# A decoder layer whose ring of gathered expert rows borrows tiles that are not yet in use

## The chip, the cores and the metric

The kernel runs on one core of one Trainium2 chip. The metric is the device time of one execution in microseconds (us); less is better. Several runs of the same program are listed and their median counts.

## The reference

The reference is one layer of a decoder for 512 tokens of 1024 features, in 32-bit floats. Its first half mixes tokens by two groups of heads: sparse attention over a shared latent, where an indexer chooses 128 keys for each query, and a gated linear recurrence in chunks of 32 tokens. An output projection, a residual and a layer norm follow; the result is called h here. Its second half is a product-key layer of 16384 experts, each of one neuron: every token chooses 16 experts for each of 8 heads, 128 in all.

```python
def _peer(x, w_q, sub_keys, u, v):
    ...
    def one_block(xb):
        q = (xb @ w_q).reshape(PEER_BLOCK, PEER_HEADS, 2, PEER_KEY_DIM // 2)
        s = jnp.einsum('thpd,hpkd->thpk', q, sub_keys).astype(jnp.float32)
        s_top, i_top = lax.top_k(s, K)
        ...
        best, pos = lax.top_k(cand.reshape(PEER_BLOCK, PEER_HEADS, K * K), K)
        experts = jnp.take_along_axis(...)
        g = jax.nn.softmax(best, axis=-1).astype(xb.dtype)
        h = jax.nn.gelu(jnp.einsum('td,thkd->thk', xb, u[experts]))
        return jnp.einsum('thk,thkd->td', g * h, v[experts])
    ...
def reference(...):
    ...
        h = _layer_norm(ALPHA * x + mix, ln1_g[layer], ln1_b[layer])
        ffn = _peer(h, peer_w_q[layer], peer_sub_keys[layer], peer_u[layer], peer_v[layer])
        x = _layer_norm(ALPHA * h + ffn, ln2_g[layer], ln2_b[layer])
```

## The kernel before

The 512 tokens are four blocks of 128, a token on each partition. `stage([0])` computes the mixing half and the choice of experts for block 0 alone; `stage([1, 2, 3])` does the same for the other three blocks together. Blocks 0 and 1 get their experts by gathering: row k of a block is a tile of 128 x 1024 floats (512 KB) that holds, for each of the 128 tokens, its k-th expert's line of `u` or `v`. Blocks 2 and 3 are computed densely against all experts at the end (`dense`): 128 steps stream all of `u` and `v` through TensorE.

**Rows.** `gather` (L625) takes a tile from the ring "g" of four buffers (`GB = 4`) and lets POOL issue an indirect DMA into it. `peer_gather(b)` (L645) gathers 128 rows of `u`, each multiplied with h and summed by one DVE instruction (L651), and then rows of `v`, each added to the block's sum by one DVE instruction (L664): 128 + 76 rows for block 0, since 52 of its `v` rows go to TensorE later (`pe_gather`), and 128 + 128 for block 1. These DVE instructions are pinned by `keep_in_program_order` behind the DVE instruction traced just before them. `pump(n)` works off n rows at fixed places of the program; the table `PUMP` gives n for each place. In `stage([1, 2, 3])` the places before the mixing norm pump 8 (cw) + 16 (qi) + 24 (sel) + 60 (the four projections of the recurrence) + 30 (hgrn) + 8 (qa) + 24 (att) = 170 rows of block 0; the mixing norm pumps 8 more, and the first quarter of the queries the last 26. Then come 14 rows on TensorE, 38 more in the dense stage, and the rows of block 1, spread over the dense loop.

**Tiles that the change touches.** The pool `cst` lives as long as the kernel. `hsA` and `hsB` (L169, L170) hold x, then h, of two blocks each: 2 x 4 KB on each partition. `hTh` (L171) and `hTl` (L865) are the high and low parts of h transposed, for blocks 2 and 3, 8 KB each; `hTl` takes the place of `hsB` once h is transposed. `mix_norm` (L470) loads x of its blocks by SP (L474), multiplies by the output weights `wo` in two halves (L486), adds (L489) and norms. For blocks 1 to 3 the homes of x are empty until then, and that of `hTh` until the queries are done (L869, L870).

**What sets the order.** All instructions are traced in program order; then a planner with a timing model of its own lays them out, engine by engine, taking the earliest traced instruction that its model holds ready. A tile's buffer must be released by all users of its last tenant before a new tenant is written. Each engine and each DMA queue then runs its list in order: POOL the gathers, SP all other loads, waiting at the head of the list where need be.

Of the kernel before, what the change touches and what calls it, by code (L numbers as in the profile page):

```python
# [9 lines left out]
F32 = mybir.dt.float32  # L10
# [14 lines left out]
DENSE = (2, 3)  # L25
# buffers of the rings of tiles
HGB = 5
# [6 lines left out]
PJ = 16  # L34
# rows of experts worked off at each such place of the program (sel: one at every second step)
PUMP = {"cw": 4, "qi": 4, "hf": 4, "hq": 4, "hi": 4, "hg": 3, "qa": 2, "hgrn": 1, "att": 4, "mix": 1, "sel": 2,
        "q0": 7, "q1": 0, "q2": 0, "q3": 0}
# rows of block 0's sum that the tensor engine takes: after the queries, and beside the dense weights
PEK1 = 14
PEK2 = 38  # L40
PEPRE = 8
PEG = 60
# tokens of each four whose weights ScalarE multiplies in
GACTS = (3, 4)
# a row of experts at every so manyth group of the dense weights
GPUMP = 3
# the dense step by which all rows are worked off
DLAST = 127
# [3 lines left out]
def tile_decoder_layer(ctx, tc, a, out):  # L52
# [70 lines left out]
    def layer_norm(ys, os_, g, b, nm):  # L123
        """Each y is a tile or a list of its parts along the features."""
        n = len(ys)
        mv = cst.tile([128, n, 2], F32, name="mv" + nm, tag="ln_mv", bufs=2)
        parts = [y if isinstance(y, list) else [y[:, k * 512:(k + 1) * 512] for k in range(2)] for y in ys]
        for i in range(n):
            st = cst.tile([128, 2, 6], F32, name=f"st{nm}_{i}", tag="ln_st", bufs=2)
            for k in range(2):  # L130
                nc.vector.bn_stats(st[:, k, :], parts[i][k])  # L131
            nc.vector.bn_aggr(mv[:, i, :], st)
        ve = cst.tile([128, n], F32, name="ve" + nm, tag="ln_ve", bufs=2)
        nc.vector.tensor_scalar(ve, mv[:, :, 1], EPS, None, op0=ALU.add)
        r = rsqrt(ve, n, nm)
        for i, o in enumerate(os_):
            if isinstance(ys[i], list):
                for k in range(2):
                    sl = slice(k * 512, k * 512 + 512)
                    nc.vector.scalar_tensor_tensor(o[:, sl], parts[i][k], mv[:, i, 0:1], g[:, sl],  # L140
                                                   op0=ALU.subtract, op1=ALU.mult)
            else:
                nc.vector.scalar_tensor_tensor(o, ys[i], mv[:, i, 0:1], g, op0=ALU.subtract, op1=ALU.mult)  # L143
            nc.vector.scalar_tensor_tensor(o, o, r[:, i:i + 1], b, op0=ALU.mult, op1=ALU.add)  # L144
# [23 lines left out]
    kiT = pre.tile([128, 512], F32, name="kiT")  # L168
    hsA = cst.tile([128, 2, 1024], F32, name="hsA")  # L169
    hsB = cst.tile([128, 2, 1024], F32, name="hsB", tag="hsB")  # L170
    hTh = cst.tile([128, 8, 256], F32R, name="hTh")  # L171
    hs = [hsA[:, 0, :], hsA[:, 1, :], hsB[:, 0, :], hsB[:, 1, :]]
    idx = [[cst.tile([128, 64], U32, name=f"idx{b}_{n}") for n in range(2)] for b in range(2)]
# [5 lines left out]
    def tok_major(blocks, xT, w, name):  # L179
        """x W for each block, tokens on partitions."""  # L180
        ps_ = [bank(f"{name}{b}") for b in blocks]
        n = w.shape[-1]
        step = 2 if n == 512 else 4
        for k0 in range(0, 8, step):
            wt = stream(f"{name}w{blocks[0]}_{k0}", w[:, k0:k0 + step, :])
            pump(PUMP[name])
            for i in range(len(blocks)):
                for k in range(step):
                    nc.tensor.matmul(ps_[i][:, :n], xT[:, k0 + k, i * 128:(i + 1) * 128], wt[:, k, :],
                                     start=(k0 + k == 0), stop=(k0 + k == 7))  # L190
        return ps_

    def feat_major(blocks, xT, w, name):
        """(x W)^T for all blocks at once, features on partitions: a bank for each 128 features."""
        m = w.shape[-1] // 128
# [22 lines left out]
    def lower_bound():  # L218
# [6 lines left out]

        # lower bound of the forget gate: f = fa + fc * tanh(z / 2)
        fa = pre.tile([128, 512], F32, name="fa")
# [41 lines left out]
    def hgrn(b, pr, mixT):  # L269
# [35 lines left out]
        for par in range(2):  # L305
            ap_ = bank(f"at{b}_{par}", "hg")
            for j in range(4):
# [3 lines left out]
                                    tri[:, None, :].to_broadcast([128, 4, 128]), op=ALU.mult)  # L311
        # the states before each chunk of 32
        S = []
# [86 lines left out]
    def select(b, pr):  # L400
        """What to add to the negated attention scores of the keys that the index doesn't choose."""
        nk = (b + 1) * 128
# [67 lines left out]
    def mix_norm(blocks, mixT):  # L470
        ys = {}
        for b in blocks:
            ys[b] = hs[b]
            tc.keep_in_program_order(nc.sync.dma_start(ys[b], a["x"][b * 128:(b + 1) * 128, :]))  # L474
# [18 lines left out]
    def queries(blocks, hT):  # L493
        """Sub-key scores and, for each of the 16 lists, its 16 best."""
        nt = 128 * len(blocks)
# [53 lines left out]
    def best16(b, g, sv, si, bv, pos):  # L549
        # a pair (a, b) can be among the 16 best only if (a + 1) * (b + 1) <= 16; the places keep the pairs' order  # L550
        s4 = sv[:, g * 4:g * 4 + 4, :].rearrange("p (h z) k -> p h z k", z=2)
# [15 lines left out]
    def routing(b, half, sv, si, bv, pos):  # L567
        """The experts and their weights for four of the block's heads."""
        H = slice(half * 4, half * 4 + 4)
        C = slice(half * 64, half * 64 + 64)  # L570
        # place -> the two ranks
        p2 = pos[:, H, :].rearrange("p h k -> p (h k)")
# [20 lines left out]
        nc.vector.tensor_copy(rbb, t1)  # L593
        # rank -> sub-key
        si4 = si.rearrange("p (h z) k -> p h z k", z=2)
# [18 lines left out]
        if b not in DENSE:  # L614
            nc.vector.scalar_tensor_tensor(idx[b][half], val[1], 128.0, val[0], op0=ALU.mult, op1=ALU.add)
        # softmax over the 16 kept, whose first is their maximum
        g3 = gate[:, b, C].rearrange("p (h k) -> p h k", h=4)
# [5 lines left out]
        nc.vector.tensor_tensor(g3, g3, gsum[:, :, None].to_broadcast([128, 4, 16]), op=ALU.mult)  # L623

    def gather(table, b, k, nm):  # L625
        t = gat.tile([128, 1024], F32, name=f"g{nm}{b}_{k}", tag="g", bufs=GB)
        nc.gpsimd.indirect_dma_start(out=t, out_offset=None, in_=table,  # L627
                                     in_offset=bass.IndirectOffsetOnAxis(ap=idx[b][k // 64][:, k % 64:k % 64 + 1], axis=0))
        return t
# [15 lines left out]
    def peer_gather(b):  # L645
        """Yields True after each row of experts is worked off, False where it waits for pe_gather."""
        hd = cst.tile([128, 128], F32, name=f"hd{b}", tag="hd")
# [24 lines left out]
    def pe_gather(n, p):  # L672
        """A part of block 0's sum over the rows of v on the tensor engine: diag(weight) @ rows; yields after each."""
        while 0 not in weighted:
# [27 lines left out]
    def dense(den, dps):  # L702
        """Tokens of the DENSE blocks against every expert, with the experts' weights scattered to a dense matrix."""
        nb = len(DENSE)
        T = 128 * nb
        tr = {}
        hTl = consts_loaded["hTl"]
        for i, b in enumerate(DENSE):
# [56 lines left out]
        def into_hidden(j, n, hp):  # L765
# [3 lines left out]
            for q, (ut, ht) in enumerate(((uh, hTl), (uh, hTh), (ul, hTh))):  # L769
                for k in range(4):  # L770
                    nc.tensor.matmul(hp, ut[:, k * 128:(k + 1) * 128], ht[:, n * 4 + k, :],  # L771
                                     start=(n + q + k == 0), stop=(n == 1 and q == 2 and k == 3))
# [20 lines left out]
        def residual():  # L793
            ia = gat.tile([128, 128], F32, name="ia", tag="dg", bufs=1)
            nc.scalar.mul(ia, ident, ALPHA)
            for i in range(nb):
                for n in range(2):
                    for c in range(4):
                        for t in (hTl, hTh):
                            nc.tensor.matmul(acc[i][n][:, c * 128:(c + 1) * 128],  # L800
                                             t.bitcast(F32)[:, n * 4 + c, i * 128:(i + 1) * 128], ia,
                                             start=False, stop=False)
# [29 lines left out]
    def stage(blocks, xT):  # L832
# [31 lines left out]
        if blocks != [0]:  # L864
            hTl = cst.tile([128, 8, 256], F32R, name="hTl", tag="hsB")  # L865
            consts_loaded["hTl"] = hTl
            for k in range(0, 8, 2):
                x = hT[:, k:k + 2, 128:384]
                nc.scalar.copy(hTh[:, k:k + 2, :], x)  # L869
                nc.vector.tensor_tensor(hTl[:, k:k + 2, :], x, hTh[:, k:k + 2, :].bitcast(F32), op=ALU.subtract)  # L870
            for _ in pe_gather(PEK1, [bank(f"pv{i}", "hg") for i in range(2)]):
                pass
# [56 lines left out]
```

## Time and profile before

| | us |
|---|---|
| three runs | 1656.95, 1659.08, 1651.08 |
| median | 1656.95 |
| profiled execution, first to last instruction (span) | 1647.0 |
| PE, DVE, ACT, POOL busy in it | 1456.9, 1387.7, 706.5, 663.7 |

For the profiled execution the page gives the span alone; its time by the clock of the runs isn't listed, and the median lies 9.95 us above the span. The engines are PE (TensorE), DVE (VectorE), ACT (ScalarE), POOL (GpSimd) and SP (SyncE, which issues DMAs). In the page's 40 slices of 41 us a digit is a share in tenths:

```profile
PE   8889899763577899868998999999999999999996
...
DVE  4139899787787669998887899998999899999998
...
POOL 0003423456665251135443344443444345534540
PEclk9899899755599999989999999999999999999998
DMA  7377878788887785246677999999999999999995
```

Block 0's stage ends at about 140 us (slice 4). Up to slice 16 the other three blocks are projected, selected, run through recurrence and attention and normed, with block 0's rows in between; then come queries, routing and the scatter of weights, and from slice 21 the dense loop. A busy share says how full an engine is, not what sets the end; for that one asks each engine what ended its idle time.

### The profile page before, as it was taken

The page shows a single profiled execution, that of the slowest core. Times are in us where ns is not written, and L with a number is a line of the kernel's source. Part 1 is how long each engine was busy: PE and PEld are TensorE (multiplying, and loading weights), DVE is VectorE, ACT ScalarE, POOL GpSimd, SP SyncE. Part 2 cuts the span into 40 slices and gives each one's busy share as a digit, 9 for nine tenths or more (in the row PEclk, how much of TensorE's full clock was granted, in tenths as well). Part 3 has the DMA queues.
Part 4 walks back from the last instruction along what each step waited for, and adds up shares of the span by engine and source line. Part 5 has one row for each costly group of instructions (what it writes and reads, how often), then busy time and mean ns, then how long its engine had stood idle before and what let it go on. Part 6 is the DMA issues. An engine that isn't in the chain of part 4 may idle for free. (4 is left out here: it accounts for less than half of the span.)

```text
span 1647.0 us, 24505 instructions
## 1 busy us (share of the span) xinstructions
PE 1456.9 (88%) x7858; PEld 1096.3 (67%) x7858; DVE 1387.7 (84%) x3263; ACT 706.5 (43%) x1501; POOL 663.7 (40%) x531
## 2 busy tenths in 40 slices
PE   8889899763577899868998999999999999999996
PEld 4567444542333365425667888888888889989885
DVE  4139899787787669998887899998999899999998
ACT  3312321122233010327996555555555555555553
POOL 0003423456665251135443344443444345534540
PEclk9899899755599999989999999999999999999998
DMA  7377878788887785246677999999999999999995
GB/s 284 122 275 248 280 265 290 245 273 275 262 276 252 264 306 186 84 136 226 220 218 263 327 345 351 355 345 344 343 356 344 336 347 359 365 349 345 354 358 191
DMA packets 166161, 467.89 MB, mean 284 GB/s; under 512 B 18576, under 2 KB 18704, under 8 KB 165904
## 3 DMA queue, kind: packets, MB, share of 16 engines
q0 software_dynamic: 73728, 268.47, 48.0%
q1 hardware_dynamic: 92304, 197.86, 33.2%
q8 instruction: 62, 1.02, 0.2%
q14 instruction: 67, 0.55, 0.1%
HBM read 464.16 MB, written 2.10 MB: 283 GB/s over the span
## 5 line engine op out<-in xcount | busy, mean ns | idle before, releaser
L627 POOL DMA_INDIRECT gv<-in_v_dram,idx x256 | 335.1, 1309 | 420.0 <-DVE hsA L664 268.6
L627 POOL DMA_INDIRECT gu<-in_u_dram,idx x256 | 318.6, 1245 | 458.2 <-DVE gu L651 289.3
L651 DVE SCALAR_TENSOR_TENSOR gu<-gu,hsA 128x1024 f32<-128x1024 f32 x256 | 309.5, 1225 | 52.5 <-DMA gu<-in_u_dram,idx 51.9
L664 DVE SCALAR_TENSOR_TENSOR hsA<-gv,gate,hsA 128x1024 f32<-128x1024 f32 x204 | 261.6, 1282 | 30.0 <-DMA gv<-in_v_dram,idx 26.6
L760 ACT CAST v_0h<-v 128x512 fp32r<-128x512 f32 x128 | 79.7, 622 | 96.7 <-PE acc L791 55.4
L518 PE MATMUL pq<-hT,wpq 128*128 128x128 f32 (+1 forms) x512 | 118.8, 390 | 0.0
L760 ACT CAST v_1h<-v 128x512 fp32r<-128x512 f32 x128 | 79.5, 621 | 88.6 <-DMA v<-in_v_dram 45.7
L762 DVE TENSOR_TENSOR u_0l<-u,u_0h 128x512 fp32r<-128x512 f32 x128 | 88.5, 692 | 32.7 <-ACT u_0h L760 29.9
L760 ACT CAST u_0h<-u 128x512 fp32r<-128x512 f32 x128 | 79.4, 620 | 72.2 <-PE hp L771 40.1
L791 PE MATMUL acc<-v_0h,wl 128*128 128x512 f32 x256 | 101.9, 398 | 2.5 <-DVE wl L781 2.5
L518 PEld LDWEIGHTS pq<-hT,wpq 128*128 128x128 f32 x512 | 80.0, 198 | 32.1 <-issue 1.7
L762 DVE TENSOR_TENSOR v_1l<-v,v_1h 128x512 fp32r<-128x512 f32 x128 | 87.8, 686 | 15.8 <-ACT v_1h L760 13.5
L791 PE MATMUL acc<-v_0h,wh 128*128 128x512 f32 x256 | 101.0, 394 | 0.0
L791 PE MATMUL acc<-v_1h,wl 128*128 128x512 f32 x256 | 99.7, 389 | 0.0
L791 PE MATMUL acc<-v_1h,wh 128*128 128x512 f32 x256 | 99.7, 389 | 0.0
L791 PE MATMUL acc<-v_0l,wh 128*128 128x512 f32 x256 | 99.5, 390 | 0.0
L760 ACT CAST u_1h<-u 128x512 fp32r<-128x512 f32 x128 | 79.4, 621 | 46.4 <-PE acc L791 42.3
L735 DVE TENSOR_TENSOR og<-iota,dtr 128x512 f32<-128x512 f32 x128 | 81.6, 687 | 13.6 <-PE gb L744 11.7
L762 DVE TENSOR_TENSOR u_1l<-u,u_1h 128x512 fp32r<-128x512 f32 x128 | 87.8, 686 | 5.1 <-ACT wh L779 2.7
L762 DVE TENSOR_TENSOR v_0l<-v,v_0h 128x512 fp32r<-128x512 f32 x128 | 88.0, 688 | 3.4 <-ACT v_0h L760 2.1
L682 PE MATMUL pw<-gv,dg 128*128 128x512 f32 x152 | 76.0, 623 | 15.6 <-ACT dg L680 9.1
L771 PE MATMUL hp<-hTl,u_0h 128*128 128x256 f32 x512 | 84.3, 287 | 5.8 <-ACT u_0h L760 5.8
(282 smaller groups left out, 3166.6 us busy)
## 6 DMA issues: line engine op xcount, KB each, us to landing
v<-in_v_dram SPq DMA_DIRECT2D x256, 256.0 KB
u<-in_ut_dram SPq DMA_DIRECT2D x256, 256.0 KB
wpq<-in_w_pq_dram SPq DMA_DIRECT2D x32, 512.0 KB
wo<-in_w_o_dram SPq DMA_DIRECT2D x16, 512.0 KB
hfw<-in_w_hf_dram SPq DMA_DIRECT2D x8, 512.0 KB
hqw<-in_w_hq_dram SPq DMA_DIRECT2D x8, 512.0 KB
hiw<-in_w_hi_dram SPq DMA_DIRECT2D x8, 512.0 KB
qaw<-in_w_qa_dram SPq DMA_DIRECT2D x8, 512.0 KB
```

The source lines that it names most:

```text
L518: nc.tensor.matmul(qp[:, :nt], w[:, k, :], hT[:, k, :nt], start=(k == 0), stop=(k == 7))
L627: nc.gpsimd.indirect_dma_start(out=t, out_offset=None, in_=table, in_offset=bass.IndirectOffsetOnAxis(ap=idx[b][k // 64][:, k % 64:k % 64 ...
L651: nc.vector.scalar_tensor_tensor(g, g, 1.0, hs[b], op0=ALU.mult, op1=ALU.mult, accum_out=hd[:, k:k + 1]))
L664: nc.vector.scalar_tensor_tensor(hs[b], g, gate[:, b, k:k + 1], hs[b], op0=ALU.mult, op1=ALU.add))
L682: nc.tensor.matmul(p[i], dg, g[:, i * 512:(i + 1) * 512], start=(k == ks[0]), stop=(k == ks[-1]))
L735: nc.vector.tensor_tensor(og[n], iota[:, None, :].to_broadcast([128, 4, 128]), x[n][:, c:c + 4, None].to_broadcast([128, 4, 128]), op=ALU. ...
L760: nc.scalar.copy(h, x)
L762: nc.vector.tensor_tensor(l, x, h.bitcast(F32), op=ALU.subtract)
L771: nc.tensor.matmul(hp, ut[:, k * 128:(k + 1) * 128], ht[:, n * 4 + k, :], start=(n + q + k == 0), stop=(n == 1 and q == 2 and k == 3))
L791: nc.tensor.matmul(acc[i][n], wt[:, sl], vt, start=(j == 0 and q == 0), stop=(j == 127 and q == 2))
```

## The change

The ring may use more buffers while they are free. x of blocks 1 to 3 and the two halves of `hTh` become single tiles of 4 KB with tags of their own, and their homes are allocated at the start. `gather` counts its calls and goes round four buffers of "g" and the homes in the list `lent`: nine until the mixing norm of blocks 1 to 3 takes back `hs1` to `hs3`, six until the queries are done, then four. `hTh` and `hTl` are lists of two halves each; `hTl`'s are in the homes of `hs2` and `hs3`. The memory used stays the same, 24 KB on each partition. Comments go, too.

```diff
-    hsA = cst.tile([128, 2, 1024], F32, name="hsA")
-    hsB = cst.tile([128, 2, 1024], F32, name="hsB", tag="hsB")
-    hTh = cst.tile([128, 8, 256], F32R, name="hTh")
-    hs = [hsA[:, 0, :], hsA[:, 1, :], hsB[:, 0, :], hsB[:, 1, :]]
+
+    hs = [cst.tile([128, 1024], F32, name="hs0")]
+    hT_parts = {}
+    lent = ["hs1", "hs2", "hs3", "hx0", "hx1"]
+    for tag in lent:
+        cst.tile([128, 1024], F32, name=tag + "_home", tag=tag)
...
         for b in blocks:
+            if b:
+                lent.remove(f"hs{b}")
+                hs.append(cst.tile([128, 1024], F32, name=f"hs{b}", tag=f"hs{b}"))
             ys[b] = hs[b]
             tc.keep_in_program_order(nc.sync.dma_start(ys[b], a["x"][b * 128:(b + 1) * 128, :]))
...
+    nth = [0]
+
     def gather(table, b, k, nm):
-        t = gat.tile([128, 1024], F32, name=f"g{nm}{b}_{k}", tag="g", bufs=GB)
+        n = nth[0] % (GB + len(lent))
+        nth[0] += 1
+        if n < GB:
+            t = gat.tile([128, 1024], F32, name=f"g{nm}{b}_{k}", tag="g", bufs=GB)
+        else:
+            t = cst.tile([128, 1024], F32, name=f"g{nm}{b}_{k}", tag=lent[n - GB])
...
-        hTl = consts_loaded["hTl"]
+        hTh, hTl = hT_parts["h"], hT_parts["l"]
...
-                    nc.tensor.matmul(hp, ut[:, k * 128:(k + 1) * 128], ht[:, n * 4 + k, :],
+                    nc.tensor.matmul(hp, ut[:, k * 128:(k + 1) * 128], ht[n][:, k, :],
...
         if blocks != [0]:
-            hTl = cst.tile([128, 8, 256], F32R, name="hTl", tag="hsB")
-            consts_loaded["hTl"] = hTl
+            lent.clear()
+            for part, tags in (("h", ("hx0", "hx1")), ("l", ("hs2", "hs3"))):
+                hT_parts[part] = [cst.tile([128, 4, 256], F32R, name=f"hT{part}{i}", tag=tag) for i, tag in enumerate(tags)]
             for k in range(0, 8, 2):
                 x = hT[:, k:k + 2, 128:384]
-                nc.scalar.copy(hTh[:, k:k + 2, :], x)
-                nc.vector.tensor_tensor(hTl[:, k:k + 2, :], x, hTh[:, k:k + 2, :].bitcast(F32), op=ALU.subtract)
+                th, tl = [hT_parts[part][k // 4][:, k % 4:k % 4 + 2, :] for part in "hl"]
+                nc.scalar.copy(th, x)
+                nc.vector.tensor_tensor(tl, x, th.bitcast(F32), op=ALU.subtract)
```

## Rows read from the trace of the kernel before

**Rows 1.** Busy by stage: start:end, length; PE, PEld, DVE, ACT, POOL; clock, DMA, GB/s.

```profile
140.00:300.00 160.00, 148.50 (x426) 77.17 (x425) 145.64 (x404) 37.39 (x72) 63.33 (x57) 0.95 0.76 259
...
300.00:450.00 150.00, 84.42 (x614) 56.34 (x612) 117.47 (x247) 32.75 (x101) 86.66 (x77) 0.59 0.83 277
...
450.00:540.00 90.00, 68.58 (x242) 34.04 (x242) 70.78 (x94) 31.60 (x65) 53.44 (x48) 0.90 0.81 271
...
540.00:618.00 78.00, 71.91 (x224) 39.79 (x224) 53.92 (x85) 9.83 (x19) 32.28 (x27) 0.96 0.79 280
...
618.00:745.00 127.00, 100.79 (x308) 52.34 (x306) 125.82 (x803) 29.95 (x59) 32.72 (x26) 0.93 0.42 134
...
865.00:1605.00 740.00, 725.26 (x4586) 652.67 (x4587) 677.98 (x1116) 401.35 (x782) 331.59 (x233) 1.00 0.96 344
```

**Rows 2.** DVE's waits (total, times, longest): 140-300, 300-450, 450-540 twice, 540-650 us.

```profile
DVE gu L651 <- DMA gu<-in_u_dram,idx: 12.6, 10, 2.4
...
DVE gu L651 <- DMA gu<-in_u_dram,idx: 31.9, 38, 3.4
...
DVE hsA L664 <- DMA gv<-in_v_dram,idx: 10.1, 17, 1.6
...
DVE gu L651 <- DMA gu<-in_u_dram,idx: 1.4, 2, 0.8
...
DVE hsA L664 <- DMA gv<-in_v_dram,idx: 16.5, 15, 2.5
```

**Rows 3.** The page's costliest groups: the two kinds of gathered row on DVE.

```profile
L651 DVE SCALAR_TENSOR_TENSOR gu<-gu,hsA 128x1024 f32<-128x1024 f32 x256 | 309.5, 1225 | 52.5 <-DMA gu<-in_u_dram,idx 51.9
...
L664 DVE SCALAR_TENSOR_TENSOR hsA<-gv,gate,hsA 128x1024 f32<-128x1024 f32 x204 | 261.6, 1282 | 30.0 <-DMA gv<-in_v_dram,idx 26.6
```

**Rows 4.** POOL's longest wait between 300 and 450 us.

```profile
POOL gu L627 <- DVE gu L651: 40.1, 38, 4.0
```

**Rows 5.** Timeline, start and duration: one buffer's row, next gather, that gather's row.

```profile
402.31 1.23 DVE L651 SCALAR_TENSOR_TENSOR gu<-gu,hsA 128x1024 f32<-128x1024 f32 x1 [0.68 <-DMA gu<-in_u_dram,idx]
...
403.81 0.94 POOL L627 DMA_INDIRECT gu<-in_u_dram,idx  x1 [0.75 <-DVE gu L651]
...
410.70 1.23 DVE L651 SCALAR_TENSOR_TENSOR gu<-gu,hsA 128x1024 f32<-128x1024 f32 x1 [1.06 <-DMA gu<-in_u_dram,idx]
```

**Rows 6.** DMA: gather queue and issues at 300-450; GB/s in 40 slices of 540-618.

```profile
q0 software_dynamic: 10803, 39.33, 79.1%
...
gu<-in_u_dram,idx POOLq DMA_INDIRECT x75
...
GB/s 95 34 303 397 393 387 340 429 403 305 235 2 88 269 260 330 128 53 216 181 107 235 233 363 296 258 277 340 372 399 414 420 372 319 275 315 327 282 343 405
```

**Rows 7.** PE's longest wait between 300 and 450 us.

```profile
PE hoT_ps L211 <- DVE o L356: 28.7, 2, 24.8
```

**Rows 8.** Rows at L664 in 618-745: start:end, length; DVE busy; clock, DMA, GB/s.

```profile
618.00:745.00 127.00, 8.12 (x7) 0.93 0.42 134
```

**Rows 9.** Timeline of SP's issues: x of block 1, output weights, their last two.

```profile
268.48 0.43 SPq L474 DMA_DIRECT2D hsA<-in_x_dram  x1
...
271.54 52.64 SPq L155 DMA_DIRECT2D wo<-in_w_o_dram  x6
...
542.98 2.04 SPq L155 DMA_DIRECT2D wo<-in_w_o_dram  x2
```

**Rows 10.** Timeline of DVE: row 166, then rows 167 to 169.

```profile
529.07 1.28 DVE L664 SCALAR_TENSOR_TENSOR hsA<-gv,gate,hsA 128x1024 f32<-128x1024 f32 x1
530.38 3.93 DVE L664 SCALAR_TENSOR_TENSOR hsA<-gv,gate,hsA 128x1024 f32<-128x1024 f32 x3
```

**Rows 11.** Timeline of PE: the last four products with the output weights.

```profile
539.53 29.17 PE L486 MATMUL mix<-wo,mixT 128*128 128x512 f32 x64 [1.46 <-DVE mixT L468]
```

**Rows 12.** Timeline of DVE: the first subtraction that splits h.

```profile
579.36 0.69 DVE L870 TENSOR_TENSOR hTl<-hT,hTh 128x512 fp32r<-128x512 f32 x1
```

More of the change, by code (lines that the diff above doesn't have):

```diff
@@ L800, in residual @@
                             nc.tensor.matmul(acc[i][n][:, c * 128:(c + 1) * 128],
-                                             t.bitcast(F32)[:, n * 4 + c, i * 128:(i + 1) * 128], ia,
+                                             t[n].bitcast(F32)[:, c, i * 128:(i + 1) * 128], ia,
                                              start=False, stop=False)
```

## The prediction

> **What bounds the kernel now.** I read the table of busy time by stage first. From 865 us to 1605 us the dense loop runs: PE is busy 725 of 740 us and the DMA engines 0.96 of the time at 344 GB/s [rows 1]. There the ring keeps its four buffers, so I expect that stage to move as a block and not to shrink. The change can only act between 140 us, where the first gathers start, and about 620 us, where the last row of block 0 is near. In that stretch no engine is full: DVE has 145.6 of 160, 117.5 of 150, 70.8 of 90 and 53.9 of 78 us [rows 1]. From 140 to 540 us that is 333.9 us of work in 400.
>
> Next I read what DVE waits for there. Nearly all of its idle time ends with the landing of a gathered row: 12.6, 31.9, 11.5 (10.1 and 1.4) and 16.5 us, 72.5 us together [rows 2]; the page's groups say the same for the whole run, 52.5 and 30.0 us before the two kinds of row [rows 3]. POOL, which issues the gathers, has its longest wait of 300-450 us, 40.1 us in 38 pieces, for DVE to give back a buffer [rows 4]. So each side waits for the other, and the loop between them is the ring. One turn of it stands in the timeline: a row is worked off from 402.31, its buffer's next gather is issued at 403.81, and that gather's row starts, waiting, at 410.70 [rows 5]. That is 8.39 us for a buffer, and with four buffers 2.10 us for a row. DVE needs less: 117.5 us of all its work for 75 rows is 1.57 us for each [rows 1, 6].
>
> Does DVE's time there reach the end? PE's longest wait in 300-450 us is 28.7 us for DVE's step in the recurrent heads [rows 7]; PE is busy 84 of 150 us at a granted clock that averages 0.59, between its two levels [rows 1]. So DVE with its rows sets the pace from 300 to 540 us, PE nearly does from 140 to 300 us (148.5 of 160 us), and the rest of the program follows behind. A saving there shifts everything later by as much.
>
> **The change part by part.** No arithmetic is added or removed: the rows, the products and the bytes stay. What changes is how many gathers may be on their way, and what must wait for a lent buffer.
>
> *Nine buffers, 140 to 540 us.* By the numbers of pumps in the source, 170 rows come before the mixing norm. The same turn of 8.39 us over nine buffers is 0.93 us for a row, below the 1.57 us that DVE needs, so the ring itself no longer limits. Two things can: DVE's work and the transfers. Between 300 and 450 us all DVE work is 117.5 us, which allows 32 us less; the waits there are 31.9 [rows 1, 2]. The stretch moves 277 GB/s for 150 us, 41.55 MB; at the dense loop's 344 GB/s that takes 121 us, which allows 29 [rows 1]. Single slices of about 2 us reach 429 GB/s [rows 6], so 344 isn't a hard end. I take three quarters of the waits, **-24 us**, since small steps of the recurrence will show waits of their own once the rows no longer cover them; the bounds are -10 (the rival of transfers, below) and -31.9. Between 450 and 540 us the waits are 11.5 us, but PE works 68.6 of 90 us through short links of the attention; I take **-7**, bounds 0 and -11.5. Between 140 and 300 us PE leaves 11.5 us idle [rows 1] and DVE waits 12.6 [rows 2]; I take **-5**, bounds 0 and -11.5.
>
> A rule of the Trainium skill speaks against this. Its page "DMA: Bandwidth & Descriptors", section "Anatomy of one DMA — SWDGE (gpsimd) path", describes a transfer issued by POOL as a fixed 2.0 us and its bytes over 436 GB/s, which makes an estimated 3.2 us for a gather of 512 KB. The trace shows 6.9 us from issue at 403.81 to the row at 410.70 [rows 5]. By the page's figure four buffers would nearly do and the change would bring next to nothing; I go by the trace.
>
> *Six buffers, after the mixing norm.* From 540 to 650 us DVE waits 16.5 us for rows [rows 2], while PE is nearly full (71.9 of 78 us [rows 1]), so most of these waits cost nothing where they are. But from 618 to 745 us DVE is busy 125.8 of 127 us [rows 1], and 8.1 us of that are rows of block 0 that come too late for the gaps before [rows 8]. Each row that is finished before 618 takes 1.28 us [rows 3] out of that full stretch. I take three of the six, **-4 us**, since the streamed weights share the transfers there (0.79 busy, 280 GB/s [rows 1]). Bounds 0 and -8.1.
>
> *The loads of x for blocks 1 to 3.* They were issued at 268.48, long before use [rows 9]. Now they need hs1 to hs3, which rows 166, 167 and 168 of the ring held last (row n goes to slot n mod 9, hs1 is slot 4, and 166 mod 9 is 4). In the trace of before these rows end between 530.3 and about 533 [rows 10]. The three loads move 1.5 MB, 5.6 us at 280 GB/s [rows 1]. Behind the waiting loads on SP stand the next sub-keys and the last two output weights (542.98 [rows 9]). The sums that need x come after products that start at 539.53 and run 29 us without a gap [rows 11], so the loads should just fit; the two sums of blocks 1 and 2 that move later are short steps in a stretch where DVE has room (53.9 of 78 us). I take **+2**, bounds 0 and +5.6.
>
> *The split of h.* hTh now needs hx0 and hx1, whose last rows are 202 and 203 of 204 (mod 6 they are 4 and 5), the last of all. The four subtractions at 579.36, 0.69 us each [rows 12], moved from a place where DVE waits anyway to behind the last row, into the full stretch: **+2**, bounds 0 and +2.8. The dense loop, which reads the parts, begins much later.
>
> Turning hsA and hsB into single tiles and the tables of parts change no instruction's size: 0. A changed granted clock between 300 and 450 us could give a little back where PE is not the bound: 0.
>
> The sum: -5 - 24 - 7 - 4 + 2 + 2 = **-36 us**. The profiled execution spans 1647.0 us, so 1611 after. The median of the runs shown, 1656.95, lies 9.95 above that span; carrying this over, the prediction is **1621 us**.
>
> **The rivals.** *The transfers are the bound.* For: the engines are already busy 0.76 to 0.83 from 140 to 540 us, and a gather that queues behind eight others simply lands later; no stretch before the dense loop averages over 280 GB/s. Against: 344 in the dense loop, and slices of 429. If the rate in 300-450 us rises only to 300 GB/s, 41.55 MB take 138.5 us: -11.5 there, nothing elsewhere, +2 for x: 1648 us; at 280 it is nil. *All waits go.* Every gather wait up to 540 us (56 us), and all rows leave the full stretch (8 us): 1657 - 64 + 4 = 1597 us. It needs PE to follow from 140 to 300 us. *The ring isn't what binds*, because four gathers already cover the time that one takes, and DVE's waits come from the order of its steps: 1657 us. The 40.1 us of POOL's waits [rows 4] and the turn of 8.39 us [rows 5] speak against it. It is what the figure of the Trainium skill's page "DMA: Bandwidth & Descriptors" would lead to.
>
> *Slower: the loads of x hold SP.* The planner that lays out the queues had put x ahead of the six output weights [rows 9]. If it keeps this order, SP stands until row 168 is done (about 533), and the weights are issued only then: 3.1 and 1.5 MB at 280 GB/s are 16.5 us, so the products start at 549 and not 539.5, and the two products done earlier in PE's gaps (six products, of which four are the last piece of 29.17 us, 7.3 us each [rows 11]) come on top: 9.5 + 14.5 = 24 us, with all of the norms behind. Against it: a queue ordered by readiness issues the weights first, since all six were issued by 324 us. With the whole gain of the rows this gives 1621 + 24 = 1645; it turns the change into a loss once the rows gain less than 24 us, and with the transfers as the bound (-11.5 for the rows) it gives about 1670.
>
> **How the numbers follow.** The forecast (1605 to 1640, at 1621) has 0.55, the transfers 0.19 (half of it beyond 0.5%), all waits gone 0.12, the ring not binding 0.05, the loss 0.09. Half a per cent, 8.3 us, is about what a measurement of this kernel can tell from no change. Faster is 0.55 + 0.12 + 0.09 = 0.76, the same 0.10 + 0.05 = 0.15, slower 0.09. The range reaches from 1597, the case without waits, to 1655, and so leaves out the loss, most of the case in which the ring doesn't bind and what lies beyond the fast end.
>
> **What would show it.** Right: DVE's waits for rows from the first gather to the mixing norm fall from 56 us to under 20; POOL's waits for DVE fall; DMA in the recurrent stretch rises to 0.9 and over 320 GB/s; the six output weights still precede x on SP; the last row before the dense loop ends some 40 us earlier and the dense loop keeps its 740 us. The transfers: gathers take 12 us and more from issue to landing, with waits as before. The loss: SP waits for DVE before x and the first output weights come after. I would be wrong above all if the planner orders DVE's steps otherwise, so that the recurrence waits behind rows that are now ready sooner.

## The result, and the profile after

The changed kernel takes 1613.38 us (median of 1606.46, 1612.88, 1622.3 and 1613.87) against 1654.01 us before (1646.41 to 1659.08): a ratio of 0.976, 95% interval 0.972 to 0.980, or 40.6 us. The profiled execution is the one of 1606.46 us, span 1604.6 us. The page's two groups of gathered rows (busy and mean, then idle time before them and its releaser) stand against [rows 3]:

```profile
L663 DVE SCALAR_TENSOR_TENSOR gu<-gu,hs 128x1024 f32<-128x1024 f32 x256 | 307.2, 1222 | 28.0 <-DMA gu<-in_u_dram,idx 27.8
...
L676 DVE SCALAR_TENSOR_TENSOR hs<-gv,gate,hs 128x1024 f32<-128x1024 f32 x204 | 261.4, 1281 | 9.7 <-DMA gv<-in_v_dram,idx 7.8
```

The rows cost what they did (1222 and 1281 ns); the idle time before them fell from 82.5 to 37.7 us. By stretch, VectorE's waits for rows (total, times, longest; 140-300, 300-450, 450-540 and 540-640 us) are the answer to [rows 2]:

```profile
DVE gu L663 <- DMA gu<-in_u_dram,idx: 2.8, 5, 1.0
...
DVE gu L663 <- DMA gu<-in_u_dram,idx: 8.0, 8, 2.9
...
DVE hs L676 <- DMA gv<-in_v_dram,idx: 0.6, 1, 0.6
...
DVE hs L676 <- DMA gv<-in_v_dram,idx: 7.2, 10, 1.3
```

Ahead of the mixing norm 56.0 us became 11.4. From 300 to 450 us POOL hardly waits any longer for VectorE to give a buffer back: 40.1 us in 38 pieces [rows 4] became 2.4 us in 3.

```profile
POOL gu L639 <- DVE gu L663: 2.4, 3, 0.9
```

Over the whole stretch from 140 to 540 us these waits of POOL only fell from 147.0 to 123.5 us. From 450 to 540 us they even rose, from 21.1 to 54.7 us, while VectorE waited 0.6 us for rows: there POOL has filled the ring and stands ahead of the need. The waits to judge by are the consumer's. Busy time by stage, with the columns of [rows 1]:

```profile
140.00:300.00 160.00, 151.95 (x504) 78.36 (x503) 156.40 (x415) 36.62 (x67) 82.22 (x69) 0.97 0.81 284
300.00:450.00 150.00, 92.26 (x592) 58.89 (x590) 138.87 (x269) 43.59 (x120) 117.24 (x97) 0.64 0.95 347
450.00:540.00 90.00, 74.63 (x251) 36.24 (x250) 59.85 (x111) 22.46 (x48) 29.50 (x27) 0.95 0.64 223
...
823.00:1563.00 740.00, 722.48 (x4573) 650.17 (x4573) 677.39 (x1111) 397.27 (x771) 327.54 (x234) 1.00 0.97 344
```

From 300 to 450 us VectorE does 138.9 us of work where it did 117.5, POOL works on 96 gathers instead of 77, and the transfers rise from 277 to 347 GB/s. The dense loop starts 42 us sooner (823 instead of 865) and keeps its length: from its first step og (below) to the end it takes 902.1 us, 901.5 before.

Where the time came off is read from the first starts of steps that both kernels have. The last mixT of VectorE (the step before the last output products) and the copy of the recurrence's last heads, hoT, by ScalarE stand in the rows of that tile (shortest, median and longest duration; first and last start), before and then after:

```profile
L108 ACT COPY mixT<-hoT_ps x4: 585/585/592, 65.4 to 454.6; 128x512 f32<-128x512 f32 x4
L468 DVE TENSOR_TENSOR mixT<-oT,rT x4: 684/688/691, 77.2 to 538.8; 128x512 f32<-128x512 f32 x4
```

```profile
L108 ACT COPY mixT<-hoT_ps x4: 586/586/587, 65.2 to 425.5; 128x512 f32<-128x512 f32 x4
L470 DVE TENSOR_TENSOR mixT<-oT,rT x4: 684/692/692, 75.6 to 501.6; 128x512 f32<-128x512 f32 x4
```

The heads are 29.1 us earlier, the last mixT 37.2. The next milestones are the last mixing product (568.1 before, 529.5 after), the last product of the queries (679.2, 640.5) and the first step og of the dense weights (745.5, 702.5): 38.6, 38.7 and 43.0 us earlier. The span is 42.4 us shorter. So in this pair of executions all but 5 us came off ahead of the last mixT, and all of that behind the last projection of the gate, whose last product TensorE starts at 274.3 us before and 274.4 after. It is one execution of each kernel, and the changed one was the fastest of its four; e11 below has the same order up to the last mixT and reaches it only 19.0 us ahead of 538.8.

### The profile page after: what moved, and what is told of

It is laid out like the page before. It is cut to its first block, busy times and chain, and to the rows that moved or that the text cites. A ratio compares the mean times of both kernels' runs of the same rounds, so it can differ in the third digit from the quotient of the medians.

```text
span 1604.6 us, 24491 instructions
## 1 busy us (share of the span) xinstructions
PE 1446.5 (90%) x7858; PEld 1087.4 (68%) x7858; DVE 1383.7 (86%) x3263; ACT 708.0 (44%) x1501; POOL 673.9 (42%) x531
## 5 line engine op out<-in xcount | busy, mean ns | idle before, releaser
L639 POOL DMA_INDIRECT gu<-in_u_dram,idx x256 | 330.9, 1293 | 409.8 <-DVE gu L663 259.1
L663 DVE SCALAR_TENSOR_TENSOR gu<-gu,hs 128x1024 f32<-128x1024 f32 x256 | 307.2, 1222 | 28.0 <-DMA gu<-in_u_dram,idx 27.8
L676 DVE SCALAR_TENSOR_TENSOR hs<-gv,gate,hs 128x1024 f32<-128x1024 f32 x204 | 261.4, 1281 | 9.7 <-DMA gv<-in_v_dram,idx 7.8
L783 PEld LDWEIGHTS hp<-hTl,u_0h 128*128 128x128 f32 x512 | 76.7, 189 | 20.8 <-ACT u_0h L772 12.4
L783 PE MATMUL hp<-hTh,u_1l 128*128 128x256 f32 x512 | 83.9, 286 | 5.1 <-DVE u_1l L774 5.1
```

The costliest lines, as they stand in the source:

```text
L663: nc.vector.scalar_tensor_tensor(g, g, 1.0, hs[b], op0=ALU.mult, op1=ALU.mult, accum_out=hd[:, k:k + 1]))
L676: nc.vector.scalar_tensor_tensor(hs[b], g, gate[:, b, k:k + 1], hs[b], op0=ALU.mult, op1=ALU.add))
L783: nc.tensor.matmul(hp, ut[:, k * 128:(k + 1) * 128], ht[n][:, k, :], start=(n + q + k == 0), stop=(n == 1 and q == 2 and k == 3))
```

## The experiments

The planner also put VectorE's steps in another order: 48 rows instead of 57 stand ahead of block 1's recurrent step, 84 instead of 76 ahead of block 2's, and 488 of its first 900 places differ. The new order could carry the gain as well as the buffers. Several kernels therefore tie an engine's instructions, each behind the last, to the order that one of the two kernels has. The tie adds no wait between engines.

```diff
+def pin(tc):
+    for eng, order in ORDER.items():
+        ins = [i for i in tc.nc.cur_bb.bb.instructions
+               if i.engine == getattr(mybir.EngineType, eng) and not type(i).__name__.startswith("BassTile")]
...
+        for x, y in zip(at, at[1:]):
+            tc.add_manual_dep(ins[y], ins[x].name,
+                              mybir.DependencyInfo(mybir.DependencyClass.NoSync, mybir.DependencyReason.DATA), reason="pin")
```

The table holds what the next paragraphs use. Row waits are those of VectorE from 140 to 540 us. The rows ahead are counted in VectorE's queue: ahead of the recurrent steps (AT) of blocks 1, 2 and 3, and of the last mixT. The starts of the last hoT copy, the last mixT and the first og are from the profiled execution.

```
            ratio [95%]             median   row waits  AT of 1/2/3   mixT   hoT    mixT   og     span
before      1                       1654.0   56.0       57/ 76/105    170   454.6  538.8  745.5  1647.0
after       0.976  [0.972 ,0.980 ]  1613.4   11.4       48/ 84/115    170   425.5  501.6  702.5  1604.6
e1          1.0401 [1.035 ,1.0452]  1720.7   55.9       57/ 76/105    170   449.8  534.0  743.6  1706.8
e2          1.0827 [1.0783,1.0871]  1792.3   49.7       48/ 84/115    170   517.3  607.4  829.1  1790.0
e3          1.0376 [1.0334,1.0418]  1720.1    3.0       57/ 76/105    204   428.8  564.7  755.9  1727.3
e4          0.9891 [0.984 ,0.9943]  1636.7   13.6       48/100/129    170   446.8  517.6  724.8  1632.0
e5          1.0088 [1.006 ,1.0115]  1672.3   60.7       48/ 84/115    170   470.1  555.0  772.9  1676.7
e6          0.994  [0.9914,0.9965]  1650.7    4.9       57/ 76/105    204   424.7  545.7  744.9  1649.7
e7          0.9914 [0.988 ,0.9947]  1643.7   26.0       60/ 96/131    170   452.0  529.3  739.1  1639.0
e8          0.9925 [0.9896,0.9954]  1643.9   17.3       78/121/131    170   465.8  539.3  750.2  1646.7
e9          0.987  [0.9832,0.9909]  1641.8    7.1       57/ 76/105    173   427.4  513.8  741.5  1639.7
e10         0.9767 [0.973 ,0.9805]  1624.6    3.8       48/ 84/115    170   438.7  514.6  723.5  1626.9
e11         0.9871 [0.9839,0.9902]  1637.0   12.0       48/ 84/115    170   445.0  519.8  736.8  1633.3
e12         0.9802 [0.9764,0.9839]  1625.7   15.3       59/ 78/109    170   435.6  513.7  723.9  1624.2
```

Each ratio is to runs of the kernel before on the same chip (medians 1657.8 for e1 to e4, 1657.9 for e5 to e8, 1659.9 for e9 to e12), so kernels are compared by ratio.

**e1, e2 and e3: VectorE alone tied.**

> The ring of four everywhere, as before the change; the first 900 instructions of VectorE are tied, each behind the last, to the very order that the trace of the kernel before shows. It is the control of the next two kernels: what the ties alone cost. Both theories: 1646 to 1662 us, ratio to the kernel before 0.995 to 1.005, and VectorE's waits for gathered rows up to the mixing norm near the 56 us of [rows 2].

> The ring of four everywhere, as before the change, but VectorE's first 900 instructions tied to the order that the trace of the changed kernel shows (rows of blocks 0 and 1 in the same places between the other steps). Theory A, the gain of 40.6 us comes from reads that are on the way sooner: no gain is left without the buffers, 1645 to 1675 us, and VectorE waits 50 us or more for gathered rows up to the mixing norm, since the same rows stand in places that are as close together. Theory B, the gain comes from the other order in which the planner put VectorE's steps (rows later, the recurrent step and the attention earlier: 48 rows instead of 57 ahead of block 1's recurrent step): 1605 to 1625 us with four buffers too. Both in part: 1625 to 1645 us.

> The changed kernel with its nine, six and four buffers, but VectorE's first 669 instructions (up to the sum of x and the mixing result of block 1) tied to the order that the trace of the kernel before shows. Theory A, reads sooner on the way: VectorE's waits for gathered rows up to the mixing norm fall from 56 us to under 20 us in the old order too, and the time is 1610 to 1630 us. Theory B, the order alone: 1645 to 1660 us. Both in part: 1630 to 1645 us.

The control missed: 1.040. Up to the first og it runs as before (743.6 against 745.5 us, row waits 55.9 against 56.0), and the 60 us are lost behind it, where block 1's rows were no longer held in program order: from the first og to the end it takes 963.2 us, against 904.8 and 898.2 in e6 and e9, which hold them. So the totals of these three say nothing, and only what lies ahead of og does. In e2 block 1's gate step kt waited once for ScalarE, which nothing tied:

```profile
DVE kt L338 <- ACT kt L337: 54.6, 1, 54.6
```

e3 shows one thing: in the old order nine buffers end the row waits (3.0 us) and bring the heads to 428.8, but from there to the last mixT it needs 136 us instead of 84.

**e5 and e6: all three engines tied.**

> The ring of four everywhere, and the whole order of the changed kernel's program for VectorE, ScalarE and TensorE (rows in the sequence of the ring of four). The run with VectorE alone tied left ScalarE to choose otherwise, and one step of the gate of block 1 waited 54.6 us for it; here that can't be. Theory A, the buffers carry the gain: the order alone brings nothing, VectorE waits 50 us or more for gathered rows up to the mixing norm, 1645 to 1675 us. Theory B, the order carries it: 1605 to 1625 us. Both in part: 1625 to 1645 us.

> The changed kernel's buffers, with VectorE, ScalarE and TensorE tied to the order of the kernel before up to the first sum of x and the mixing result (VectorE's first 669 steps, ScalarE's 400, TensorE's 1500); all behind that is left to the planner as in the changed kernel. With VectorE alone tied the waits for gathered rows had gone (3.0 us from 300 to 540), but ScalarE and TensorE ran in another order and VectorE waited for them. Theory A: with these tied as well VectorE's steps come sooner by the 45 us or so of waits that are gone, the last mixing matmul ends near 530 us instead of 568.1, and the time is 1605 to 1630 us. Theory B, the old order keeps the old time: the last mixing matmul near 560 us or later, 1640 to 1660 us.

Theory B falls with e5. The whole new order with four buffers is slower than the kernel before (1.0088); VectorE waits for rows as ever, 300 to 450 us:

```profile
DVE gu L871 <- DMA gu<-in_u_dram,idx: 35.2, 46, 2.4
```

By its numbers e6 is Theory B: the last mixing product starts at 575.3 us, and the time is 1650.7. But the order up to the heads isn't the reason. Its heads are there at 424.7 us, as early as in the changed kernel, and then the 29.9 us gained are spent again, and 6.9 more. The reason lies behind the tie: it ended at the 138th row, and behind it the planner put 185 and 204 rows ahead of the mixT of blocks 2 and 3, where 152 and 170 stood. 34 rows of 1.22 to 1.28 us are 42 us. From 450 to 540 us VectorE is busy 84.4 of 90 us and TensorE only 44.8:

```profile
450.00:540.00 90.00, 44.80 (x156) 21.58 (x157) 84.36 (x91) 20.89 (x46) 64.93 (x57) 0.75 0.93 346
```

**e9: the old order up to the mixing.**

> The changed kernel's buffers, with VectorE, ScalarE and TensorE tied to the order of the kernel before for all that is traced ahead of the mixing of blocks 1 to 3, and rows of gathered experts up to the 170th in their old places; 57 rows stand ahead of block 1's recurrent step, 132 and 152 ahead of the mixT of blocks 1 and 2 (as before the change), 173 ahead of block 3's (170 before). The mixing and what follows is left to the planner. In the kernel that was tied only up to the 138th row, the last hoT was copied at 424.7 us (425.5 in the changed kernel, 454.6 before), but 185 and 204 rows stood ahead of the mixT of blocks 2 and 3, and the 34 rows more at 1.22 to 1.28 us each are the 42 us that it lost behind. Theory A (buffers end the waits; the places of the rows only have to stay about where they were): last mixT between 497 and 512 us, 1608 to 1628 us. Theory C (the new order is as much the cause as the buffers): last mixT at 520 us or later, 1632 to 1655 us.

The last mixT starts at 513.8 us, 25.0 us before that of the kernel before, with old places and 3 rows more ahead of it. The changed kernel's order with nine buffers gave 501.6, 514.6 (e10) and 519.8 (e11). So the buffers bring the gain up to the mixing in either order, and the new order adds nothing that these profiles can tell from their spread. The last mixT lies between the bounds of the two theories, and the time, 1641.8 us, in Theory C's range. What was lost came behind that point, where the planner had the rest: it put the 31 rows of block 0 that were left among the steps of the mixing and its norm (204 rows stand ahead of the queries, 180 in both kernels), and TensorE waited for VectorE's norm:

```profile
564.13 1.97 PE L266 MATMUL hT_ps<-ident,hs 128*128 128x128 f32 x8 [19.64 <-DVE hs L197]
```

The queries begin 32.2 us behind the start of the last mixing product, where both kernels need 10.6. That is 21.6 of the 24.6 us by which e9 is slower than the changed kernel from there to og.

**e7, e8 and e10: half the bytes.** Block 0's rows on VectorE come from a table seen as lines of 512 numbers.

```diff
-        nc.gpsimd.indirect_dma_start(out=t, out_offset=None, in_=table,
+        w = 512 if b == 0 and rows[0] > 256 else 1024
+        nc.gpsimd.indirect_dma_start(out=t[:, :w], out_offset=None, in_=table if w == 1024 else bass.AP(tensor=table.tensor, offset=table.offset, ap=[[512, 16384], [1, 512]]),
```

> The ring of four, but each of block 0's 204 gathered rows that VectorE works off moves 2 KB a token instead of 4 KB (the first half of the table taken as lines of 512 numbers); VectorE reads that half twice, so its instruction keeps 1024 numbers a token. Part of the computation changes. It takes the bytes away and leaves the ring's depth. If a row's landing is set by the bytes of the three or four reads under way, a turn of a buffer gets shorter by about half of the landing (6.9 us to some 4 us), nearly all of the 56 us of waits go, and the time is that of the changed kernel or a little under it: 1600 to 1625 us. If a read of a row takes its 6 to 7 us whatever its bytes, the waits stay at 45 us or more: 1645 to 1660 us.

> The changed kernel with the same halved reads of block 0's rows (part of the computation changes). The rival that the transfers are the bound once the ring is deep (0.94 of the DMA engines from 300 to 400 us) expects a further gain of 15 us or more, 1585 to 1600 us. If TensorE's and VectorE's own chain is the bound after the change, at most the 19 us that VectorE still waits for rows are to be had, and less than half of them: 1603 to 1614 us.

> The changed kernel with block 0's 204 gathered rows of half the bytes (2 KB a token, VectorE reads the half twice; part of the computation changes), and VectorE, ScalarE and TensorE tied to the whole order of the changed kernel. Without the tie the planner put 121 rows instead of 84 ahead of block 2's recurrent step, which hid what the bytes do. Rival, the transfers are the bound with nine buffers: 1575 to 1598 us. My reading, the engines' own chain is the bound and at most the 19 us of waits that are left can go, less than half of them on the path: 1600 to 1614 us. What is left out of the sum would show as 1614 to 1625 us.

e7 fits neither bound: row waits fell to 26.0 us and the time by 14 us. To see how long a row was under way I paired the n-th gather on POOL with the n-th row on VectorE from 140 to 480 us and took the rows that waited: from the end of POOL's instruction to the row's start the median is 4.5 us before (63 rows, 3.2 to 14.1) and 2.5 us in e7 (47 rows, 2.3 to 8.2). So the bytes are a large part of a row's landing, and with half of them over half of the waits with four buffers are gone. The time says less, since the planner also put 20 and 26 rows more ahead of the steps of blocks 2 and 3.

e8 surprised: fewer bytes and nine buffers, yet slower than the changed kernel. There is no transfer to blame (0.52 of the DMA engines from 300 to 450 us). The planner, which saw shorter gathers, put 121 rows ahead of block 2's recurrent step instead of 84, and the heads came at 465.8 us. With the changed kernel's order tied (e10) the same halved rows give 438.7 and 0.9767, against 0.976 for full rows:

```profile
300.00:450.00 150.00, 88.08 (x580) 56.92 (x579) 131.58 (x263) 40.83 (x112) 116.14 (x92) 0.64 0.60 173
```

The transfers run at half the rate and nothing is gained: of its three readings the last came (1624.6 us, or 1615.5 if the ratio is taken of 1654.0). That refutes the rival of the transfers for the changed kernel. e8 against e10, 0.016 or 26 us, is the price of the planner's other order. The 37 rows more ahead of block 2's step are its largest difference among the counted places; that they alone cost the 26 us isn't shown.

**e11 and e12: the number of buffers.** e11 lends homes only while hs3 is free, so up to the mixing norm; e12 lends only hx0 and hx1.

```diff
-        n = nth[0] % (GB + len(lent))
+        free = lent if "hs3" in lent else []
+        n = nth[0] % (GB + len(free))
```

```diff
-        n = nth[0] % (GB + len(lent))
+        free = [t for t in lent if t[:2] == "hx"]
+        n = nth[0] % (GB + len(free))
```

> The changed kernel, but with four buffers instead of six from the mixing norm on (nine before it, as in the change). VectorE's order up to the mixing is that of the changed kernel; the split of h stands after 180 to 182 rows instead of 204. The prediction's term for the six buffers was -4 us (0 to -8.1): 1614 to 1621 us. If the six buffers bring nothing there: 1608 to 1614 us. If the split's wait for the rows (+2) weighs more than the buffers: under 1612 us.

> The changed kernel with only the two homes of x of blocks 2 and 3 lent: six buffers all along until those are claimed, no nine. The turn of a buffer in the kernel before was 8.39 us; six rows of 1.22 us take 7.3 us, so rows that stand close together would still wait about 1 us in each turn, against 3.5 us with four buffers. By that the 45 us of waits up to 540 us fall to 10 to 15 us, and the time to 1618 to 1632 us. If depth up to nine is needed to fill the transfers: 1632 to 1645 us. The planner's places for the rows are near those of the kernel before (59, 78 and 109 ahead of the recurrent steps, 57, 76 and 105 before).

e12 came as expected: six buffers give 0.980, nine 0.976, and the intervals overlap. The step from four to six is nearly all of the gain; for nine over six no gain is shown. Since e12's rows stand near their old places (59, 78 and 109), it also shows the gain without the changed kernel's order. From 300 to 450 us:

```profile
300.00:450.00 150.00, 88.89 (x605) 56.42 (x606) 133.20 (x271) 41.69 (x116) 109.96 (x89) 0.65 0.90 321
```

e11 lost 0.011 to the changed kernel, 18 us where 4 were expected. Its trace divides this. Up to the last mixT VectorE, ScalarE and TensorE run the same steps in the same order as in the changed kernel, with the same nine buffers, and still its last mixT is 18.2 us later: that is spread, not buffers. Behind it, 10.5 us are lost. Its 26 rows behind the mixing take from 556.3 to 613.5 us, with 14.0 us of waits (7.2 in the changed kernel, 538.1 to 582.2), and one gather for TensorE's own sum of rows is late (POOL's instruction, then TensorE's wait for it):

```profile
712.52 12.60 POOL L640 DMA_INDIRECT gv<-in_v_dram,idx  x1 [1.16 <-PE pw L695]
...
PE pw L695 <- DMA gv<-in_v_dram,idx: 9.7, 1, 9.7
```

The 6.8 us of row waits are in the bounds of the prediction's term (0 to 8.1). The late gather isn't the work of the four buffers: e12, with six there, has one of 10.31 us. How much of the 18 us belongs to the two buffers, and how much to that gather and to the spread, stays open.

**e4: x ahead of the output weights.**

```diff
+        if pinned:
+            tc.keep_in_program_order(d)
...
-                ws.append(stream(f"wo{blocks[0]}_{nh}_{k0}", a["w_o"][nh, :, k0:k0 + 2, :]))
+                ws.append(stream(f"wo{blocks[0]}_{nh}_{k0}", a["w_o"][nh, :, k0:k0 + 2, :], blocks != [0]))
```

> The changed kernel with one thing forced on SyncE's queue: the loads of w_o for blocks 1 to 3 stand behind the loads of x in program order, so that they can't be issued before the buffers of hx2, hx3 and the rest were given back by gathered rows. It makes the slower rival of the prediction happen. By that rival's price TensorE's mixing matmuls wait for w_o some 24 us: 1630 to 1650 us, ratio to the kernel before 0.985 to 0.998. If w_o is read from the chip's memory within the time that the mixing norm's other steps leave, or VectorE has rows to do in that time that it would have to do later: 1613 to 1625 us.

The ratio is 0.9891, 0.013 or 22 us above the changed kernel. SyncE does what the rival says: the x loads are issued at 501.78 and the six weights behind them at 504.85.

```profile
501.78 2.97 SPq L481 DMA_DIRECT2D hs<-in_x_dram  x3
504.85 3.83 SPq L155 DMA_DIRECT2D wo<-in_w_o_dram  x6
...
511.05 5.40 PE L493 MATMUL mix<-wo,mixT 128*128 128x512 f32 x8 [2.15 <-DMA wo<-in_w_o_dram]
516.72 37.93 PE L493 MATMUL mix<-wo,mixT 128*128 128x512 f32 x88
```

But the wait for weights is 2.15 us, not 9.5. What costs more is that products could no longer be done early: 88 stand in one piece of 37.93 us where the changed kernel has 64 in 27.73, 10.2 us. The rest lies ahead, in heads that come at 446.8 us and a last mixT at 517.6, 16.0 later than in the changed kernel; 100 rows instead of 84 ahead of block 2's step would explain 19.5 us (16 of 1.22), but e11 came to 445.0 with 84, so this part can't be told from spread.

## Why the prediction was right

The forecast was a sum of -36 us and a ratio of 0.978; -40.6 us and 0.976 came.

- *What binds.* Shown: the waits for rows fell from 56 to 11.4 us, POOL's waits for buffers all but ended from 300 to 450 us, and the last mixT came 37.2 us sooner. With the order alone (e5) nothing was gained, with the buffers in the old order (e9) 25 us up to that point, and with six buffers near the old order (e12) a ratio of 0.980. The sign "POOL's waits for DVE fall" was too wide: over the whole stretch they fell only from 147.0 to 123.5 us. And the rows end 72.5 of the 90.2 us in which VectorE is idle in the four stretches that I read, four fifths rather than "nearly all".
- *Nine buffers, -5, -24 and -7.* The sum, -36, stands against -37.2 at the last mixT. That they agree so closely is luck: other executions with nine buffers gained 24.2 (e10, with half the bytes) and 19.0 us (e11) there. Nor was it made where I put it. From 140 to 300 us nothing came off TensorE's chain (projections end at 274.4, 274.3 before); the -5 came as 0 on that chain. The buffers only let POOL work on 66 gathers instead of 54, so rows were ahead. The gain showed behind, 29.1 us up to the last heads and 8 more in the attention. And nine was not needed: e12 has nearly all of it with six. My step "a turn of 8.39 us over nine buffers" had the same answer at six (1.40 us for a row, below VectorE's 1.57), and I did not work that out.
- *Six buffers, -4.* From the last mixing product to og the changed kernel needs 173.0 us instead of 177.4, with the +2 for the split of h in it; -4.4 for the -2 of the sum. One pair of executions doesn't show that: with six buffers others needed 170.7 (e4), 179.3 (e10) and 182.3 us (e12), with four 181.9 (e7) and 189.2 (e11). All of block 0's rows left the full stretch (the last starts at 582.2, 632.9 before), where I had let three of six go.
- *x on SP, +2.* VectorE waited 1.0 us for x. SyncE kept the six output weights ahead, at 269.82 us, as I had argued; the loads of x follow at 492.88.

```profile
269.82 36.51 SPq L155 DMA_DIRECT2D wo<-in_w_o_dram  x6
492.88 2.97 SPq L479 DMA_DIRECT2D hs<-in_x_dram  x3
```

- *The 9.95 us carried over* from span to median was the wrong step. A time lies 1.9 us over its span (1606.46 and 1604.6); the rest was the spread of the times, in which the profiled execution lay low. With 1.9 us the prediction would have been 1613.
- *The rivals.* Transfers as the bound: refuted by e10; nor did its sign come, since the gathers of the changed kernel landed 6.2 to 6.3 us after issue in the median from 140 to 450 us, not 12 and more. Ring not binding, which the figure of the Trainium skill's page "DMA: Bandwidth & Descriptors" would lead to: refuted by e12, where two more buffers give 0.980. x ahead of the weights: real when forced, and my 24 us met 22 by luck, with its two terms mis-sized (9.5 came as 2.15, 14.5 as 10.2) and the rest unexplained.
- *"I would be wrong above all if the planner orders DVE's steps otherwise".* It did order otherwise, harmlessly here. e6, e8 and e9 show that the danger was real: 34 rows more ahead of the last mixT spent the whole gain up to there (e6, whose total is 0.994), 24 rows more ahead of the queries made these 21.6 us later (e9), and the other order of e8 cost 26 us.

## What to carry to other kernels

Where a consumer and its gathers wait for each other, take the turn of one buffer from the timeline, divide it by the work per piece, and add buffers only to that number; here six did what nine do. More buffers give time to whoever stands next in the queue, so look at how many pieces the planner then puts ahead of the steps on the critical chain, since each counts with its full duration. Before trusting one profile's milestones, compare two executions of the same order.

## What the runs showed of the hardware

The same order of steps up to the mixing, with the same full rows and nine buffers, put its last hoT at 425.5 us in one execution and at 445.0 in another (e11). Four times of the changed kernel range over 16 us. From 350 to 375 us both had a granted clock of 0.50, the lower level of 1.2 GHz; from 400 to 425 us the quicker one had 0.64 and the slower one 0.50. The clock there can explain the last part of the 19.5 us at most, since the last recurrent step AT, at 390.5 and 401.9 us, already lay 11.4 us apart. Where those come from stays open.

A gather's instruction on POOL, 0.93 us at its shortest, took 12.60 us in e11 and 10.31 in e12. In e11 it began at 712.52 and ended at 725.12, while VectorE ran the short steps of the routing, among them many bf16 products and sums (L612 to L617), back to back up to 724.83. In the changed kernel the longest there took 4.24 us and ended at 702.25, 0.3 us after VectorE's run:

```profile
698.01 4.24 POOL L639 DMA_INDIRECT gv<-in_v_dram,idx  x1 [1.02 <-PE pw L694]
...
701.72 0.23 DVE L620 SCALAR_TENSOR_TENSOR idx<-dc_v,dc_v 128x64 uint32<-128x64 f32 x1
```

The Trainium skill's page "SBUF — State Buffer", section "SBUF: two separate sides", says that a transfer issued by GpSimd can't write its descriptors while VectorE runs a step in a two-port mode. The traces agree in that the gather ends when VectorE's run does: in 11 of the 14 traces such a gather ends 0.3 us behind the last step of the run. Which of VectorE's steps use that mode they don't show, and no run here removed the steps to prove it. In e9 and e12 the gather lies on the chain of work that ended last, here in e12:

```profile
704.54 14.55 DMA gv<-in_v_dram,idx
...
719.23 3.75 PE pw L695 x4
```

So a gather that TensorE needs may be better issued before such a run; no run here tried it.
